# Low parts of 64 weight units: a subtraction on VectorE replaced by an adding transfer out of main memory

## The chip, the cores and the metric

One Trainium2 chip, one core. Its engines run side by side: TensorE (matmuls, PE in the profile), VectorE (DVE), ScalarE (ACT), GpSimd (POOL) and SyncE (SP), the last three also issuing transfers that 16 DMA engines carry out. The metric is the time of one execution in device microseconds; the kernel before takes 1455.31 us (median of three runs).

## The reference

One layer of an encoder for 256 tokens of width 2048, in float32: a normalisation, one wide input projection, two kinds of attention, two gates, two branch projections, an output projection, a gated MLP with a width-3 convolution, a gated extra embedding, and a last normalisation. Cut to its products:

```python
h = rms_norm(x, attn_norm)
qa, ka, va, qb, kb, vb, ga, gb = split(h @ w_in)
ya, yb = windowed_gqa(qa, ka, va), dilated_attention(qb, kb, vb)
x = x + (sigmoid(ga) * (ya @ w_branch_a) + sigmoid(gb) * (yb @ w_branch_b)) @ w_out
hf = rms_norm(x, ffn_norm)
x = x + (gelu(dwconv(hf @ w_ffn_gate)) * (hf @ w_ffn_up)) @ w_ffn_down
x = x + sigmoid(rms_norm(x, ple_norm) @ w_ple_gate) * (p @ w_ple_proj)
return rms_norm(x, final_norm)
```

## The kernel before

**Weights as pieces and units.** All weights lie in main memory as `wts`: 258 pieces of 128 x 2048 float32 (1 MB each), in the order of their use. SyncE loads a piece into one of three `raw` buffers (`load`, L257; L254 and L255 for pieces of which one quarter was prepared earlier). A piece is cut into units, most of them of 1024 columns. `produce` turns a unit into two float32r tiles: a high part `hi`, which is the weights rounded by ScalarE (L305), and a low part `lo`, the weights minus `hi`, by VectorE (L306). Products are then made in three matmuls (`thirds`, L408 to L410): activations high by weights high, high by low, low by high. So a low part is first needed by the L409 matmul of its unit.

**Kinds of pieces.** `_PIECES` gives each a letter. `f`: 16 blocks of 128 x 128, used in the input projection (stage A) and in the MLP's two up-projections (E0, E1). `s`: two chunks by two column ranges, used in eight products, two units. `w`: the same with four chunks of one column range, also two units. `S` and `Z`: the same data used in seven products (a Strassen-like scheme), four units, two of them (ring `v`) being differences that VectorE makes in place in `raw` (L282, L283, L295 to L297).

**Stages behind attention.** In order: B0 to B3 (gates), each followed by ba (w_branch_a, two `w` pieces) and bb (w_branch_b, one `w` piece); D0, D1 (w_out); E0, F00, F01 (the MLP's first half: up-projections, then w_ffn_down for two column halves); E1, F10, F11 (its second half); pp0, pp1 (w_ple_proj); G0, G2, G3 (w_ple_gate). Pieces: B0 is `ssssSsSs`; B1 to B3, D0 and D1 are `SsSsSsSs`; F00 and F01 `ZZsZsZsZsZs`; F10 and F11 `ZsZsZsZsZss`; G0 `ZsZsZsZs`; G2 and G3 are `w` pieces; pp0 and pp1 one `s` piece each.

**Order.** Units go through two rings, six of kind `u` and two of kind `v`. When TensorE has used a unit for the last time, `drop` gives its place free and `pump` produces the next units in order. A planner at build time then fixes each engine's instruction order by the expected readiness of instructions; `keep` pins an instruction behind what its engine was given before. At the start of a stage VectorE and ScalarE also finish the stage before (L890 to L894, L1005, L1007, L1009; turning back of rows, L512 and L513).

**GpSimd's queue** holds little: in E0 and E1, transfers that prepare quarters of `Z` pieces (`ahead`: 52 loads of 384 KB, L268, and 52 stores of 128 KB, L275), and three square roots (L528) for the normalisations.

Of the kernel before, what the change touches and what calls it, by code (L numbers as in the profile page):

```python
# [10 lines left out]
F32 = mybir.dt.float32  # L11
FR = mybir.dt.float32r
AF = mybir.ActivationFunctionType
ALU = mybir.AluOpType
# [149 lines left out]
_PIECES, _STAGES = _pieces()  # L164
# [3 lines left out]
def _unit_list():  # L168

    units, of = [], []  # L170
    for p, (kind, _) in enumerate(_PIECES):
        if p == 0:
            cuts = [("n", a * P, b * P) for a, b in ((0, 1), (1, 4), (4, 7), (7, 11), (11, PIECE))]
        elif kind == "Z":
            cuts = [("n", WIDE, 2 * WIDE), ("n", 2 * WIDE, 4 * WIDE), ("T21", 0, 2 * WIDE), ("T03", 2 * WIDE, 4 * WIDE)]
        elif kind == "S":
            cuts = [("n", 0, WIDE), ("n", 2 * WIDE, 4 * WIDE), ("T13", 0, 2 * WIDE), ("T24", 2 * WIDE, 4 * WIDE)]
        else:
            cuts = [("n", 0, 2 * WIDE), ("n", 2 * WIDE, 4 * WIDE)]
        of.append(list(range(len(units), len(units) + len(cuts))))  # L180
        units += [(p, *cut) for cut in cuts]
    return units, of


_UNITS, _UNITS_OF = _unit_list()
_FBLOCKS = [(u, o) for p, (kind, _) in enumerate(_PIECES) if kind == "f" for u in _UNITS_OF[p]
            for o in range((_UNITS[u][3] - _UNITS[u][2]) // P)]
_LAST_OF = {u: o for u, o in _FBLOCKS}
# [5 lines left out]
def _encoder(ctx: ExitStack, tc, xt, pt, xrow, cols, gainrow, table, onehot, mask, ident_in, wts, out):  # L194
    nc = tc.nc
# [12 lines left out]
    def bank(which, *shape):  # L208

        if which in RING:  # L210
            n = turns.get(which, 0)
            turns[which] = n + 1
            which = RING[which][n % len(RING[which])]
        else:
            which = BANK[which]
        return ps.tile(list(shape) or [P, 2 * T], F32, name="bank", tag="b%d" % which, bufs=1)
# [33 lines left out]
    def load(r, a=0, b=PIECE):  # L250
        if a == 0:
            raws[r] = wpool.tile([P, PIECE * P], F32, name="raw", bufs=3)
        if _PIECES[r][0] == "Z":
            nc.sync.dma_start(raws[r][:, WIDE:], wts[r][:, WIDE:])  # L254
            nc.sync.dma_start(raws[r][:, :WIDE], ahead.pop(r))  # L255
        else:
            nc.sync.dma_start(raws[r][:, a * P:b * P], wts[r][:, a * P:b * P])  # L257
        state["raw"] = r + 1
# [20 lines left out]
    def sums_of_weights(raw):  # L279

        q = [raw[:, i * WIDE:(i + 1) * WIDE] for i in range(4)]
        nc.vector.tensor_tensor(q[1], q[0], q[1], op=ALU.subtract)  # L282
        nc.vector.tensor_tensor(raw[:, 2 * WIDE:], raw[:, 2 * WIDE:], view(q[0], 0, (0, 2), (1, WIDE)), op=ALU.subtract)  # L283

    def produce():

        u = state["unit"]
        p, kind, a, b = _UNITS[u]
        while state["raw"] < min(p + 3, _NPIECES):
            load(state["raw"])  # L290
        raw = raws[p]
        ring = "u" if kind == "n" else "v"
        if kind == "T13":
            q = [raw[:, i * WIDE:(i + 1) * WIDE] for i in range(4)]
            nc.vector.tensor_tensor(raw[:, :2 * WIDE], raw[:, WIDE:3 * WIDE], raw[:, :2 * WIDE], op=ALU.subtract)  # L295
            nc.vector.tensor_tensor(q[2], q[2], q[0], op=ALU.subtract)
            nc.vector.tensor_tensor(q[3], q[3], q[2], op=ALU.subtract)  # L297
        behind = _PIECES[p][0] == "Z" == _PIECES[p - 1][0]
        if kind == "T21" and not behind:
            sums_of_weights(raw)  # L300
        src = raw[:, a:b]
        pool = wpool if ring == "u" else held["tok"]
        hi = pool.tile([P, b - a], FR, name=ring + "h", bufs=RINGS[ring])
        lo = pool.tile([P, b - a], FR, name=ring + "l", bufs=RINGS[ring])
        nc.scalar.activation(hi, src, AF.Copy)  # L305
        nc.vector.tensor_tensor(lo, src, hi.bitcast(F32), op=ALU.subtract)  # L306
        if behind and u == _UNITS_OF[p][1]:
            sums_of_weights(raw)
        made[u] = (hi, lo)
        state["unit"] = u + 1  # L310
        state[ring] -= 1

    def pump():
        while not state["early"] and state["unit"] < len(_UNITS):
            p, kind = _UNITS[state["unit"]][:2]
            if state["u" if kind == "n" else "v"] <= 0 or kind != "n" and "tok" not in held:
                break
            produce()

    def weights(u):  # L320
        while state["unit"] <= u:
            produce()
        return made[u]
# [167 lines left out]
    keep = tc.keep_in_program_order  # L491
# [148 lines left out]
    for step in order:  # L640
        if len(step) == 3:
            produce()
        else:
            for k in range(*step):
                gained(hs[:, k, :], x[:, k, :], gain(0, k))
            ready = step[1]
        while state["at"] < min(FIRST * ready, _EARLY[state["unit"]]):
            k, e = divmod(state["at"], FIRST)
            block(firsts[e], hs[:, k, :], k == 0, k == KC - 1)
        while 4 * done + 9 < state["at"] // FIRST:  # L650
            square(done)
            done += 1
# [16 lines left out]
    b = bank("misc", NH, 2 * T)  # L669
# [470 lines left out]
    for half in range(2):  # L1140
# [3 lines left out]
        stage = "E%d" % half  # L1144
# [87 lines left out]
    for t in range(2):  # L1232
        for h in range(2):
            cols = slice(3 * WIDE + h * T, 3 * WIDE + (h + 1) * T)
            u, r = c[t][:, WIDE + h * T:WIDE + (h + 1) * T], xr[:, t, cols]
# [72 lines left out]
```

## Time and profile before

| | |
|---|---|
| runs | 1454.77, 1455.31, 1455.72 us |
| span of the profiled execution, first to last instruction | 1453.7 us |
| TensorE busy, matmuls | 1442.7 us (99%) |
| VectorE busy | 1220.8 us (84%) |
| ScalarE busy | 829.6 us (57%) |
| GpSimd busy | 73.8 us (5%) |
| granted TensorE clock, mean | 0.997 |
| mean transfer rate | 213 GB/s |
| read from main memory | 299.94 MB |

The profile is one execution on the chip; for it only the span is recorded, and the runs' times hold 1.6 us more than that span at their median, which lies around the instructions. "Busy" is the time in which at least one instruction of an engine runs. Lines such as L306 are lines of the kernel. In rows of a timeline stand the start in us, the duration in us, the engine, the line, the operation, output and inputs, and in brackets the idle time before it with what ended it. In the list of waits stand the total, the count and the longest. In the windows stand the stretch, its length and each engine's busy time with its count, then the granted clock, the share of the DMA engines and GB/s.

### The profile page before, as it was taken

What the parts mean: (1) busy time and instruction counts of PE and PEld (TensorE: products, weight loads), DVE (VectorE), ACT (ScalarE), POOL (GpSimd) and SP (SyncE); (2) the same over time, 40 slices, a digit from 0 to 9 for tenths busy, and PEclk for the clock granted to TensorE, in tenths of its full rate; (3) what the DMA queues carried; (4) which work ended last, traced back from release to release, by engine and by line L of the source; (5) the groups of instructions that cost most, each with busy time, mean ns of one, the idle gap of its engine ahead of it and who ended that gap; (6) DMA issues with size and microseconds to landing.
All of it is one profiled execution on the core that took longest, in us unless ns stands there. A gap on an engine that the chain in (4) does not pass through costs nothing.

```text
span 1453.7 us, 19747 instructions
## 1 busy us (share of the span) xinstructions
PE 1442.7 (99%) x7470; PEld 1234.0 (85%) x7470; DVE 1220.8 (84%) x1730; ACT 829.6 (57%) x1148; POOL 73.8 (5%) x113
## 2 busy tenths in 40 slices
PE   9999999999999999999999999999999999999997
PEld 8888888888888888888888888888888888888885
DVE  7677665679998989989877999997878799998994
ACT  7455544546555656566545566465545466555753
POOL 0000000000000000000221100000121200000000
PEclk9999999999999999999999999999999999999998
DMA  9753445435456456465767655566776765556462
GB/s 330 252 209 146 155 167 175 172 143 203 189 190 231 180 210 239 178 253 203 277 238 267 241 208 198 189 248 227 263 275 243 271 236 213 197 194 233 173 236 82
DMA packets 58522, 310.17 MB, mean 213 GB/s; under 512 B 7028, under 2 KB 12020, under 8 KB 29500
## 3 DMA queue, kind: packets, MB, share of 16 engines
q1 hardware_dynamic: 49388, 280.46, 53.1%
q0 software_dynamic: 8320, 27.27, 5.2%
q8 instruction: 58, 0.95, 0.3%
q10 hardware_dynamic: 720, 1.19, 0.2%
q14 instruction: 36, 0.29, 0.1%
HBM read 299.94 MB, written 8.95 MB: 212 GB/s over the span
## 4 chain that ended last, share of the span: by engine, by line
PE 98%; DMA 0%; issue 0%; DVE 0%; ACT 0%; SPq 0%; POOLq 0%; POOL 0%; DVEq 0%
PE bank L351 29%; PE bank L358 15%; PE bank L408 15%; PE bank L409 14%; PE bank L410 14%; PE bank L397 2%; PE bank L399 2%; PE bank L398 2%; PE bank L335 2%; PE bank L336 1%; PE bank L939 1%; PE bank L755 0%; PE bank L703 0%; PE bank L702 0%; PE bank L701 0%; DMA raw<-in_wts 0%
## 5 line engine op out<-in xcount | busy, mean ns | idle before, releaser
L305 ACT ACTIVATE uh<-raw 128x1024 fp32r<-128x1024 f32 (+2 forms) x519 | 518.1, 1010 | 297.0 <-PE bank L410 106.5
L306 DVE TENSOR_TENSOR ul<-raw,uh 128x1024 fp32r<-128x1024 f32 (+2 forms) x519 | 594.4, 1164 | 96.5 <-ACT uh L305 65.9
L351 PE MATMUL bank<-hf,uh 128*128 128x512 f32 x1408 | 336.3, 391 | 0.0
L351 PEld LDWEIGHTS bank<-hf,uh 128*128 128x128 f32 x1408 | 258.9, 188 | 50.1
L358 PEld LDWEIGHTS bank<-hf,ul 128*128 128x128 f32 x1408 | 180.4, 191 | 6.7
L358 PE MATMUL bank<-hf,ul 128*128 128x256 f32 x1408 | 182.8, 283 | 0.0
L305 ACT ACTIVATE vh<-raw 128x1024 fp32r<-128x1024 f32 x96 | 101.1, 1058 | 59.8 <-DVE raw L282 27.0
L306 DVE TENSOR_TENSOR vl<-raw,vh 128x1024 fp32r<-128x1024 f32 x96 | 116.3, 1220 | 1.1
L351 PE MATMUL bank<-hs,uh 128*128 128x512 f32 x432 | 103.6, 392 | 0.0
L351 PEld LDWEIGHTS bank<-hs,uh 128*128 128x128 f32 x432 | 79.5, 188 | 15.6
L410 PE MATMUL bank<-uh,act 128*128 128x512 f32 x218 | 84.9, 390 | 0.0
L409 PE MATMUL bank<-ul,act 128*128 128x512 f32 x218 | 84.8, 389 | 0.0
L408 PE MATMUL bank<-uh,act 128*128 128x512 f32 x218 | 84.6, 390 | 0.0
L496 ACT ACTIVATE t<-bank 128x256 f32<-128x256 f32 x122 | 45.3, 374 | 59.8 <-PE bank L358 48.7
L408 PE MATMUL bank<-uh,hs 128*128 128x512 f32 x172 | 67.4, 392 | 0.0
L410 PE MATMUL bank<-uh,hs 128*128 128x512 f32 x172 | 67.2, 391 | 0.0
L409 PE MATMUL bank<-ul,hs 128*128 128x512 f32 x172 | 67.0, 389 | 0.0
L1084 ACT ACTIVATE gw<-gw,cl 128x256 f32<-128x256 f32 x44 | 24.0, 594 | 72.2 <-DVE gw L1081 71.9
L271 DVE TENSOR_TENSOR ahead<-ahead 128x256 f32<-128x256 f32 x52 | 21.9, 422 | 46.8 <-DMA ahead<-in_wts 46.8
L268 POOL DMA_DIRECT2D ahead<-in_wts x52 | 39.0, 750 | 375.7 <-DMA ahead<-ahead 207.0
L358 PE MATMUL bank<-hs,ul 128*128 128x256 f32 x432 | 56.6, 284 | 0.0
L358 PEld LDWEIGHTS bank<-hs,ul 128*128 128x128 f32 x432 | 54.5, 191 | 1.0
(266 smaller groups left out, 2423.8 us busy)
## 6 DMA issues: line engine op xcount, KB each, us to landing
raw<-in_wts SPq DMA_DIRECT2D x225, 1024.0 KB, 4.9
ahead<-in_wts POOLq DMA_DIRECT2D x52, 384.0 KB, 5.2
raw<-in_wts SPq DMA_DIRECT2D x26, 768.0 KB, 5.1
ahead<-ahead POOLq DMA_DIRECT2D x52, 128.0 KB, 4.4
raw<-ahead SPq DMA_DIRECT2D x26, 256.0 KB, 4.9
raw<-in_wts SPq DMA_DIRECT2D x12, 512.0 KB, 7.0
xr<-in_xrow SPq DMA_DIRECT2D x4, 512.0 KB, 8.4
x<-in_xt SPq DMA_DIRECT2D x13, 128.0 KB, 6.0
```

The lines of the kernel that those rows point to most:

```text
L268: keep(nc.gpsimd.dma_start(q, wts[p][:, :3 * WIDE].rearrange("p (q c) -> p q c", c=WIDE)[:, :, cols]))
L305: nc.scalar.activation(hi, src, AF.Copy)
L306: nc.vector.tensor_tensor(lo, src, hi.bitcast(F32), op=ALU.subtract)
L335: nc.tensor.matmul(acc, hi[:, w], m, start=first, stop=False, skip_group_check=True)
L351: nc.tensor.matmul(acc, weights(u)[0][:, o * P:(o + 1) * P], m, start=first, stop=False, skip_group_check=True)
L358: nc.tensor.matmul(acc[:, T:], weights(u)[1][:, o * P:(o + 1) * P], m[:, :T], start=False, stop=last, skip_group_check=True)
L397: nc.tensor.matmul(acc[:, :n * P], xh, hi, start=(k == 0), stop=False)
L398: nc.tensor.matmul(acc[:, :n * P], xh, lo, start=False, stop=False)
L408: nc.tensor.matmul(acc, sh, wh, start=first, stop=False)
L409: nc.tensor.matmul(acc, sh, wl, start=False, stop=False)
L410: nc.tensor.matmul(acc, sl, wh, start=False, stop=last)
L496: keep(nc.scalar.activation(t, acc[:, T:], AF.Copy, scale=scale))
```

## The change

The second unit (columns 1024 to 2047) of every `s` and `w` piece in the stages B, ba, bb, D, F and G0 is treated in another way, 64 units in all. ScalarE writes the negated rounding of the weights into the low part's tile, and then the rounding into the high part's tile. A transfer issued by GpSimd then reads the same 1024 columns (512 KB) once more out of main memory and adds them to what is in the low part's tile. VectorE's subtraction falls away for them. All other units stay as they were, and so do all matmuls.

```diff
+_MOVED = {_UNITS_OF[p][1] for stage in _STAGES if stage[0] in "BbDFG" and stage not in ("G2", "G3")
+          for p in _STAGES[stage] if _PIECES[p][0] in 'sw'}
...
         hi = pool.tile([P, b - a], FR, name=ring + "h", bufs=RINGS[ring])
         lo = pool.tile([P, b - a], FR, name=ring + "l", bufs=RINGS[ring])
-        nc.scalar.activation(hi, src, AF.Copy)
-        nc.vector.tensor_tensor(lo, src, hi.bitcast(F32), op=ALU.subtract)
+        if u in _MOVED:
+            nc.scalar.activation(lo, src, AF.Copy, scale=-1.0)
+            nc.scalar.activation(hi, src, AF.Copy)
+            keep(nc.gpsimd.dma_start(lo, wts[p][:, a:b], accum_op=ALU.add))
+        else:
+            nc.scalar.activation(hi, src, AF.Copy)
+            nc.vector.tensor_tensor(lo, src, hi.bitcast(F32), op=ALU.subtract)
```

## The prediction, made before the changed kernel ran

> **What bounds the kernel now.** I read the page first, then TensorE's list of waits, then the windows of the stages that the change touches, then the times of single units. The page:
>
> ```profile
> span 1453.7 us, 19747 instructions
> PE 1442.7 (99%) x7470; PEld 1234.0 (85%) x7470; DVE 1220.8 (84%) x1730; ACT 829.6 (57%) x1148; POOL 73.8 (5%) x113
> PEclk9999999999999999999999999999999999999998
> PE 98%; DMA 0%; issue 0%; DVE 0%; ACT 0%; SPq 0%; POOLq 0%; POOL 0%; DVEq 0%
> ```
>
> The chain that ended last is TensorE for 98% of the span. A busy TensorE may hide short waits, since ends of matmuls are modelled, so the list of waits and the starts count:
>
> ```profile
> PE bank L234 <- DVE mhalf L229: 1.1, 1, 1.1
> PE bank L336 <- DVE ul L306: 0.2, 1, 0.2
> ...
> 402.15 0.39 PE L409 MATMUL bank<-ul,hs 128*128 128x512 f32 x1
> 402.38 0.39 PE L410 MATMUL bank<-uh,hs 128*128 128x512 f32 x1
> 402.60 0.39 PE L408 MATMUL bank<-uh,S 128*128 128x512 f32 x1
> ```
>
> Two waits in the whole execution, 1.3 us together, both before the touched stages; and in them one 512-column matmul starts 0.23 us after the last. Nothing that makes VectorE lighter can bring much: there is hardly a wait to take away. What can change the time is a new wait. The touched stages are gates and branch projections (B, ba, bb), w_out (D), the two w_ffn_down stages (F) and the first w_ple_gate stage (G0):
>
> ```profile
> 350.00:620.00 270.00, 270.00 (x1208) 221.13 (x1207) 254.28 (x304) 163.19 (x187) 0.00 (x0) 1.00 0.54 199
> 850.00:985.00 135.00, 135.00 (x632) 112.63 (x631) 126.00 (x143) 78.61 (x93) 0.00 (x0) 1.00 0.56 207
> 1225.00:1400.00 175.00, 175.00 (x800) 145.06 (x799) 162.86 (x202) 107.77 (x138) 1.08 (x1) 1.00 0.57 206
> ...
> 620.00:850.00 230.00, 230.00 (x1314) 202.49 (x1313) 194.28 (x320) 130.82 (x196) 32.63 (x49) 1.00 0.69 249
> ```
>
> Columns: PE, PEld, DVE, ACT, POOL busy, clock, DMA share, GB/s. VectorE is busy 543 of 580 us there, ScalarE 350, GpSimd 1.1. The fourth row is the first MLP stage, untouched, where GpSimd's own transfers run today.
>
> **The change part by part.** By the piece patterns, 64 units move: 18 in B, 8 in ba, 4 in bb, 8 in D, 22 in F, 4 in G0.
>
> *Removed:* 64 subtractions on VectorE of 1.22 us (next start 1.14 us later). 64 x 1.14 = 73 us off its 543. On TensorE's path that is worth 0 by the waits above. I do not count the few short delays among them.
>
> *Added on ScalarE:* 64 rounded negations of 1.05 us, 67 us on 350, so it is busy 72%. The negation comes first, where the rounding stood, so the low part's first half is ready when the high part was; the high part comes 1.05 us later. The piece's buffer is free after two ScalarE passes instead of one pass and a lagging subtraction, so SyncE's next load does not start later.
>
> *Added to the DMA engines:* 64 x 512 KB = 33.6 MB in 580 us, 58 GB/s on about 203. In proportion to the share that is 0.55 to 0.71 as plain transfers; the first MLP stage ran at 0.69 and 249 GB/s with no wait of TensorE. So bandwidth is no bound; latency may be.
>
> *Added wait:* TensorE's first low-part matmul of such a unit waits for a transfer instead of VectorE, and all later matmuls stand behind it. The path is: negation ends, GpSimd's queue issues, the data comes and is added, TensorE may read. Before has no adding transfer. The nearest rows are GpSimd's transfers in the MLP stages:
>
> ```profile
> L268 POOL DMA_DIRECT2D ahead<-in_wts x52: 741/743/929, 638.8 to 1168.4; - x52
> DMA to landing us min/median/max: 3.3/4.8/6.5
> ...
> ahead<-in_wts POOLq DMA_DIRECT2D x52, 384.0 KB, 5.2
> ahead<-ahead POOLq DMA_DIRECT2D x52, 128.0 KB, 4.4
> ```
>
> From 128 to 384 KB costs 0.8 us, so 0.4 us per 128 KB over a fixed 4.0 (one of the two is a store, so this is rough). A plain 512 KB would take 4.0 + 1.6 = 5.6 us. Adding must also read what lies in the destination: if that doubles the moving part, 7.2; if it triples it, 8.8. Below, 4.8, the median over both kinds. I take 6.0, nearest to the plain row, because the DMA share is 0.55 in these stages and 0.69 where the row was taken. Ends kept: 4.8 and 8.8.
>
> The Trainium skill, page "DMA: Bandwidth & Descriptors", section "Anatomy of one DMA — SWDGE (gpsimd) path", fits a transfer from GpSimd as 2.0 us plus its bytes at 436 GB/s, which is 3.2 us for 512 KB (an estimate by that page); by it no unit below would be late and the sum is 0. The trace disagrees on its own case: the fit gives 2.9 us for the 384 KB that took 5.2.
>
> *Cover:* how long after the end of the rounding (in the changed kernel, of the negation) TensorE first needs the low part. I matched ScalarE's L305 roundings in order to units, and units to TensorE's matmuls. The tightest and the widest of the 64, one in the steady run of stage B, and those that decide:
>
> ```profile
> 947.07 1.04 ACT L305 ACTIVATE uh<-raw 128x1024 fp32r<-128x1024 f32 x1
> 951.63 0.39 PE L409 MATMUL bank<-ul,act 128*128 128x512 f32 x1
> ...
> 302.52 1.06 ACT L305 ACTIVATE uh<-raw 128x1024 fp32r<-128x1024 f32 x1 [0.75 <-PE bank L351]
> 318.60 0.39 PE L409 MATMUL bank<-ul,hs 128*128 128x512 f32 x1
> ...
> 441.42 1.06 ACT L305 ACTIVATE uh<-raw 128x1024 fp32r<-128x1024 f32 x1 [0.45 <-PE bank L410]
> 452.33 0.39 PE L409 MATMUL bank<-ul,hs 128*128 128x512 f32 x1
> ...
> 605.72 0.46 ACT L512 ACTIVATE hf<-bank,cl 128x256 fp32r<-128x256 f32 x1
> 606.07 1.05 ACT L305 ACTIVATE uh<-raw 128x1024 fp32r<-128x1024 f32 x1
> 612.37 0.39 PE L409 MATMUL bank<-ul,merged 128*128 128x512 f32 x1
> ...
> 889.57 1.04 ACT L305 ACTIVATE uh<-raw 128x1024 fp32r<-128x1024 f32 x1
> 895.54 0.39 PE L409 MATMUL bank<-ul,act 128*128 128x512 f32 x1
> ...
> 1310.16 1.04 ACT L305 ACTIVATE uh<-raw 128x1024 fp32r<-128x1024 f32 x1
> 1315.70 0.39 PE L409 MATMUL bank<-ul,act 128*128 128x512 f32 x1
> ...
> 1357.47 1.08 ACT L305 ACTIVATE uh<-raw 128x1024 fp32r<-128x1024 f32 x1
> 1365.16 0.39 PE L409 MATMUL bank<-ul,pl 128*128 128x512 f32 x1
> ```
>
> Covers: 3.5 us (second F stage), 15.0, 9.9, 5.3 (D1), 4.9 (first F stage), 4.5 (fourth F stage), 6.6 (G0). Stage B and D0 in the steady run lie near 10: the ring of six units sets that, and 6.0 fits in. The short ones lie behind the start of a stage, where VectorE is late with sums:
>
> ```profile
> 920.66 0.69 DVE L306 TENSOR_TENSOR ul<-raw,uh 128x512 fp32r<-128x512 f32 x1 [1.79 <-ACT uh L305]
> ...
> 939.34 4.09 DVE L306 TENSOR_TENSOR ul<-raw,uh 128x1024 fp32r<-128x1024 f32 x4
> 943.35 0.69 DVE L282 TENSOR_TENSOR raw<-raw 128x512 f32<-128x512 f32 x1
> ```
>
> VectorE has no pause from 920.66 on, and the second of the four subtractions at 939.34 is of a moved unit. Without it the sums at 943.35, on which ScalarE's next units wait, come 1.14 us sooner. So the 3.5 becomes 4.66; in the first F stage one moved unit stands ahead likewise, 4.93 + 1.14 = 6.07; in the fourth F stage two, 4.5 + 2.28 = 6.8. The D1 unit sits behind ScalarE's L512 and gets nothing, 5.25; nor does the one in G0.
>
> *Sum at 6.0 us:* short by 1.34 in the second F stage and 0.75 in D1, other units not at all: +2.1 us. The profiled span becomes 1455.8. The median of the runs, 1455.31, lies 1.6 us above the span of 1453.7 (the start and end outside it), so the forecast is 1457.4. The limit of what can be told from no change is 0.2%, 2.9 us: I forecast no change that can be told, on its slow side.
>
> *Queues:* GpSimd has 1.1 us of work in these stages. The one other instruction that could meet a transfer there is the root before G0, quoted in the rivals. SyncE's loads are not moved past anything.
>
> **The rivals.**
>
> *Slower, the transfers land late.* The same units, a larger price. At 7.2 us: 2.54 + 1.95 + 1.13 + 0.42 + 0.6 (G0) = 6.6 us, 1462. At 8.8 the same five are short by 4.1, 3.6, 2.7, 2.0 and 2.2, and some units with covers of 7.4 to 8.6 by another 4: 18.6, 1474. It decides from 6.3 us on (1.64 + 1.05 + 0.23 = 2.9). For it: an addition needs the destination read too, on DMA engines that are busy more than half of the time. Against: one late unit gives the next one its delay as cover, and the order on TensorE is made by a planner that pulls high-part products ahead of a late low part. Above 10 us the steady covers break too, 64 us for each further us: 1540 at 11, with little chance.
>
> *Slower, GpSimd's queue is blocked.*
>
> ```profile
> 1361.30 1.08 POOL L528 TENSOR_TENSOR rr<-rv,mhalf 128x2 f32<-128x2 f32 x1 [183.86 <-DVE rv L526]
> ```
>
> GpSimd stands on this root's wait for 184 us. If the planner leaves it ahead of G0's first transfer, that can be issued at 1362.4 instead of 1358.6 and lands 6.0 later, 3.2 us after the use at 1365.16: 1460.6 with the sum. Against: in program order that unit is produced first. A rule of the Trainium skill points the same way for all 64: "SBUF — State Buffer", section "Who interferes with whom", says VectorE in its 2-port modes locks GpSimd out while descriptors are written. The issue times above (741 to 929 ns over 52, beside a VectorE busy 84%) show no such lock; at most one 1.2 us VectorE instruction per transfer, which is the 7.2 us case.
>
> *Hidden anyway.* At 4.8 only the unit in the second F stage is short, by 0.1: 1455.4. The fastest transfer, 3.3, speaks for it; against it, half of the transfers take longer than 4.8, and they are smaller and add nothing. (By the skill's fit above it would be this case, too.)
>
> *Faster.* VectorE's 73 us end waits that the modelled ends hide. It would take 2.9 us of them; the regular starts and the 0.2 us in the list speak against. 1452.
>
> **How the numbers follow.** Forecast (landing between 4.9 and 6.3) 0.40, hidden 0.10, late transfers 0.38, blocked queue or above 10 us 0.07, faster 0.05. Same 0.50, slower 0.45, faster 0.05. The likeliest is 1457.4. The range goes from 1454.0 (hidden, with 1.3 us gained) to 1470.0 (a landing of 8.3 us), leaving out about 1 in 10 above and less below. The forecast alone reaches from 1455 to 1458.2.
>
> **What would show it.** L306's subtractions fall from 519 to 455, L305's line splits, GpSimd gets 64 issues with a time to landing near 6 us, VectorE's busy time falls by about 73 us, ScalarE's rises by about 67. TensorE's waits name transfers into ul, a few times, about 1 us each, at 606 to 620 and 945 to 955, and none in stage B. It is wrong if stage B shows waits (landing above 10), if many of the F units do (above 8), if the clock falls from 1.00 in the touched windows, or if waits appear on high parts, which would be ScalarE's added 67 us.

## The result, and the profile after

The changed kernel takes 1556.96 us (median of 1555.10, 1556.96 and 1562.67) against 1455.31: ratio 1.0705, 95% interval 1.0676 to 1.0734. That is 101.6 us slower, far above the range of 1454.0 to 1470.0. Lines stand lower in it: L305 is now L312 (the two ScalarE passes of a moved unit are L308 and L309), L306 is L313, L408 to L410 are L415 to L417, and the new transfer is L310. The page of the changed kernel:

```profile
span 1553.3 us, 19981 instructions
PE 1472.7 (95%) x7470; PEld 1245.6 (80%) x7470; DVE 1155.1 (74%) x1666; ACT 886.1 (57%) x1212; POOL 129.4 (8%) x177
PEclk9999999999999999899999999989999999999999
...
raw<-in_wts SPq DMA_DIRECT2D x225, 1024.0 KB, 5.5
ul<-in_wts POOLq DMA_DIRECT2D x64, 512.0 KB, 9.3
...
raw<-in_wts SPq DMA_DIRECT2D x26, 768.0 KB, 8.3
```

The span grew by 99.6 us. TensorE, with the same 7470 matmuls, is busy 30.0 us longer (1472.7 against 1442.7) and pauses 69.6 us more (1553.3 - 1472.7 = 80.6 against 11.0). VectorE lost 65.7 us of work and ScalarE gained 56.5: neither total matters. The three last rows tell where to look: the new transfers take 9.3 us from issue to landing, and SyncE's loads also land later than before. Their rows on the page of the kernel before:

```profile
raw<-in_wts SPq DMA_DIRECT2D x225, 1024.0 KB, 4.9
...
raw<-in_wts SPq DMA_DIRECT2D x26, 768.0 KB, 5.1
```

What TensorE waited for in the changed kernel:

```profile
PE bank L416 <- DMA ul<-in_wts: 57.0, 26, 6.7
PE bank L415 <- DVE c L899: 5.4, 2, 2.8
PE bank L946 <- DVE merged L950: 4.5, 4, 1.9
```

Before, that list had 1.3 us in two waits. Now the landing alone ends 57.0 us in 26. Most of the rest ends with sums on VectorE, at the starts of stages above all.

The other 30 us are TensorE working more slowly. Windows over the gate and branch stages, over two of the worst places and over one untouched stage, columns as before (clock, DMA share and GB/s last):

```profile
350.00:620.00 270.00, 252.09 (x1094) 201.65 (x1093) 202.49 (x249) 167.77 (x190) 24.40 (x28) 0.99 0.81 242
...
630.00:680.00 50.00, 37.42 (x161) 29.88 (x160) 29.82 (x35) 22.99 (x29) 1.75 (x2) 0.86 0.62 196
980.00:1030.00 50.00, 41.25 (x169) 33.09 (x168) 36.62 (x39) 26.93 (x29) 3.45 (x4) 0.93 0.60 183
1060.00:1290.00 230.00, 230.00 (x1322) 203.18 (x1322) 190.09 (x315) 126.78 (x188) 35.48 (x54) 1.00 0.71 253
```

The granted clock falls to 0.86 and 0.93 where the longest pauses are and is 1.00 where there are none. In the clock records of the whole run the rate is 0.5 in 12 stretches ahead of the last one at the end, each of 3.41 or 6.83 us, 51.2 us together; work at half rate for that long costs 25.6 us. The Trainium skill's page "TensorE: Matmul & The Clock Gate", section "Part 1: The HAM clock gate (the "warmup" mystery)", says that TensorE drops to half rate after an idle window of about 3.4 us; the trace agrees in the length of the stretches, but no whole idle window is needed: every stretch begins within 5.2 us of the start of a wait, and six of the twelve waits are of only 1.9 to 2.8 us.

By stage (the shift of the same matmul between the two traces), the loss is 25.2 us in B0 to D0, 21.0 in D1, 21.8 in F00 and F01, 21.1 in F10 and F11, 10.4 in G0, and 0 in E0, E1, G2 and G3.

One late unit, the second of D1, in the timeline of the changed kernel:

```profile
618.40 1.07 ACT L309 ACTIVATE uh<-raw 128x1024 fp32r<-128x1024 f32 x1
...
623.55 1.22 DVE L313 TENSOR_TENSOR ul<-raw,uh 128x1024 fp32r<-128x1024 f32 x1
...
625.56 1.05 ACT L308 ACTIVATE ul<-raw 128x1024 fp32r<-128x1024 f32 x1
626.63 0.92 SPq L259 DMA_DIRECT2D raw<-in_wts  x2
627.01 0.86 POOL L310 DMA_DIRECT2D ul<-in_wts  x1 [18.56 <-DVE vl L313]
...
637.05 0.79 PE L416 MATMUL bank<-ul,merged 128*128 128x512 f32 x1 [6.74 <-DMA ul<-in_wts]
```

The negation runs 7.2 us after the rounding, not before it: it comes behind VectorE's subtraction for the first half (623.55). The transfer is issued 0.4 us after the negation, but 0.4 us behind the issue of a 1 MB load. Its first packet moves at 631.24, 4.2 us after the issue, the last ends at 636.69, and the landing is told at 637.00. TensorE stands for 6.74 us, and its next matmul takes 0.79 instead of 0.39 us: half rate.

### The profile page after: what moved, and what is told of

Same layout as the page of the kernel before. It is cut to its first block, busy times and chain, and to the rows that moved or that the text cites. A ratio compares the mean times of both kernels' runs of the same rounds, so it can differ in the third digit from the quotient of the medians.

```text
span 1553.3 us, 19981 instructions
## 1 busy us (share of the span) xinstructions
PE 1472.7 (95%) x7470; PEld 1245.6 (80%) x7470; DVE 1155.1 (74%) x1666; ACT 886.1 (57%) x1212; POOL 129.4 (8%) x177
## 5 line engine op out<-in xcount | busy, mean ns | idle before, releaser
L313 DVE TENSOR_TENSOR ul<-raw,uh 128x1024 fp32r<-128x1024 f32 (+2 forms) x455 | 520.5, 1157 | 229.1 <-ACT uh L312 196.4
L312 ACT ACTIVATE uh<-raw 128x1024 fp32r<-128x1024 f32 (+2 forms) x455 | 453.0, 1005 | 367.1 <-PE bank L417 126.5
L310 POOL DMA_DIRECT2D ul<-in_wts x64 | 55.9, 874 | 955.5 <-ACT ul L308 488.8
L313 DVE TENSOR_TENSOR vl<-raw,vh 128x1024 fp32r<-128x1024 f32 x96 | 116.9, 1221 | 23.8 <-ACT vh L312 23.1
L312 ACT ACTIVATE vh<-raw 128x1024 fp32r<-128x1024 f32 x96 | 100.4, 1052 | 33.3 <-DVE raw L284 12.7
L416 PE MATMUL bank<-ul,act 128*128 128x512 f32 x218 | 90.4, 415 | 24.6 <-DMA ul<-in_wts 24.6
L417 PE MATMUL bank<-uh,act 128*128 128x512 f32 x218 | 88.4, 407 | 0.0
L415 PE MATMUL bank<-uh,act 128*128 128x512 f32 x218 | 87.5, 405 | 0.0
L416 PEld LDWEIGHTS bank<-ul,act 128*128 128x128 f32 x218 | 42.9, 197 | 38.9 <-DMA ul<-in_wts 30.0
L308 ACT ACTIVATE ul<-raw 128x1024 fp32r<-128x1024 f32 x64 | 67.2, 1049 | 7.1 <-PE bank L416 4.5
L415 PE MATMUL bank<-uh,hs 128*128 128x512 f32 x172 | 68.8, 400 | 0.0
L309 ACT ACTIVATE uh<-raw 128x1024 fp32r<-128x1024 f32 x64 | 66.9, 1045 | 2.8 <-PE bank L358 2.5
L417 PE MATMUL bank<-uh,hs 128*128 128x512 f32 x172 | 68.1, 397 | 0.0
```

The source lines that it names most:

```text
L308: nc.scalar.activation(lo, src, AF.Copy, scale=-1.0)
L310: keep(nc.gpsimd.dma_start(lo, wts[p][:, a:b], accum_op=ALU.add))
L415: nc.tensor.matmul(acc, sh, wh, start=first, stop=False)
L416: nc.tensor.matmul(acc, sh, wl, start=False, stop=False)
L417: nc.tensor.matmul(acc, sl, wh, start=False, stop=last)
```

## The experiments

Times are compared with runs of the kernel before on the same chip (medians of 1455.1 to 1455.4). Diffs are against the changed kernel. Theory 1 in the expectations is that the landing of an adding transfer is longer than I took it; the others are told where they stand.

**Leaving out one part at a time.** ScalarE's two passes with VectorE's subtraction kept and no transfer:

```diff
-            keep(nc.gpsimd.dma_start(lo, wts[p][:, a:b], accum_op=ALU.add))
+            nc.vector.tensor_tensor(lo, src, hi.bitcast(F32), op=ALU.subtract)
```

> The negation and both ScalarE passes stay, but the low part is then subtracted by VectorE as before, and there is no transfer. Theory 1: no loss, 1455 to 1457 us. Theory 3 (ScalarE's added 67 us delay high parts and the buffers' release, and so the loads): a good part of the 100 us stays, over 1480 us.

Measured 1456.71 us, ratio 1.0010 (1.0000 to 1.0019). So the added ScalarE work is hidden, as predicted, and the loss lies with the transfers.

The same transfers, overwriting instead of adding (the low part then is the weights themselves, the difference is left out):

```diff
-            keep(nc.gpsimd.dma_start(lo, wts[p][:, a:b], accum_op=ALU.add))
+            keep(nc.gpsimd.dma_start(lo, wts[p][:, a:b]))
```

> The 64 transfers overwrite the low part's tile with the weights instead of adding to it; all else as in the changed kernel (the output is then not the reference's: the low parts of these units hold whole weights). Theory 1 (the addition is what is slow: 0.63 us per round of 4 KB packets, where plain ones take 0.16): landing falls from 9.3 to about 5 to 5.6 us, TensorE's waits on these transfers from 57 us to under 5, the time to 1455 to 1459 us. Theory 2 (the conversion to float32r or GpSimd's path itself is slow at 512 KB): landing stays at 8 to 10 us and the time above 1530 us.

Measured 1509.78, ratio 1.0371 (1.0338 to 1.0404). Its list of waits, and its row of the transfers:

```profile
PE bank L416 <- DMA ul<-in_wts: 23.8, 11, 5.3
```

```profile
ul<-in_wts POOLq DMA_DIRECT2D x64, 512.0 KB, 6.8
```

The adding is worth 47 us of the 101.6. A plain transfer lands 2.5 us sooner and still costs 54, so the addition is not the only term that was missed.

**Is main memory the slow part of an adding transfer?** The same addition with the weights taken from the `raw` buffer:

```diff
-            keep(nc.gpsimd.dma_start(lo, wts[p][:, a:b], accum_op=ALU.add))
+            keep(nc.gpsimd.dma_start(lo, src, accum_op=ALU.add))
```

> The adding transfer reads the weights from the raw buffer in SBUF instead of main memory. If the round of 0.63 us is the addition's own (theory 1), the transfer takes as long, 8 to 10 us to land, and the time is no better than 1555 us, worse if the buffer, held until the transfer has read it, delays the next load. If main memory's latency in the second read is what is slow, the landing falls to 5 to 6 us.

A single run took 1565.09 us. The landing is 8.2 us at the median, and a packet of 4 KB takes 327 ns with either source, where a plain one takes 159 (GpSimd's loads in the kernel before) to 174. So the source isn't what makes a packet slow. That the whole became no faster has a reason of its own: each `raw` buffer is now held until the landing. SyncE stands on these transfers 64 times there, 452.9 us in all, before it can issue a load.

**Less to move, or a later use.** Half of the columns by the transfer, the other half by VectorE:

```diff
-            nc.scalar.activation(lo, src, AF.Copy, scale=-1.0)
+            nc.scalar.activation(lo[:, WIDE:], src[:, WIDE:], AF.Copy, scale=-1.0)
...
-            keep(nc.gpsimd.dma_start(lo, wts[p][:, a:b], accum_op=ALU.add))
+            keep(nc.gpsimd.dma_start(lo[:, WIDE:], wts[p][:, a + WIDE:b], accum_op=ALU.add))
+            nc.vector.tensor_tensor(lo[:, :WIDE], src[:, :WIDE], hi[:, :WIDE].bitcast(F32), op=ALU.subtract)
```

> Only columns 512 to 1023 of each moved unit go by negation and adding transfer (256 KB), VectorE subtracts the other 512; rings as in the changed kernel. Theory 1: eight rounds of 2 KB packets, half the moving time, landing 6 to 7 us, as the plain transfers of 512 KB, so a time near theirs, 1500 to 1520 us. If packets cost the same whatever their size, landing stays near 9 us and the time near 1555 us.

Measured 1515.82, ratio 1.0417 (1.0376 to 1.0458), landing 7.3 us. Half of the bytes take away 2.0 us of the landing and 41 us of the loss. And the moved unit used in the last four of its piece's eight products, but for a stage's last piece:

```diff
                     t, n, c = g // 4, g // 2 % 2, g % 2
+                    if us[1] in _MOVED and i < len(pieces) - 1:
+                        c, t, n = g // 4, g // 2 % 2, g % 2
```

> In the eight-product pieces, but for the last of a stage, the moved unit is used in the last four products instead of every second one, so its low part is needed about 3 x 0.68 = 2.0 us later. Theory 1 with its corollary (a fixed landing against a fixed cover): the stalls in B and D0 of 0.5 to 1 us per unit vanish and those behind stage starts shrink by 2 us each: 1500 to 1520 us. Theory 4 (the DMA engines cannot supply the weights fast enough): TensorE waits in sum as long as now, 1545 to 1560 us.

Measured 1540.53, ratio 1.0580 (1.0562 to 1.0597), 44.1 us of waits on the landing in 25. That is 16 us less, and above what theory 1 gave. Not every unit got the 2 us: in three units the negation now comes 10.0 to 12.4 us after the rounding (at most 8.8 in the changed kernel). So the run agrees with landing against cover as the sum, but it is no clean step of the cover.

**Does the negation hang on VectorE through the ring?** The moved low parts get a ring of two of their own, the others keep four:

```diff
-        lo = pool.tile([P, b - a], FR, name=ring + "l", bufs=RINGS[ring])
+        if ring == "u" and u in _MOVED:
+            lo = pool.tile([P, b - a], FR, name="ml", bufs=2)
+        else:
+            lo = pool.tile([P, b - a], FR, name=ring + "l", bufs=4 if ring == "u" else RINGS[ring])
```

> The moved units' low parts get a ring of their own (two places, the other low parts four; six in all as before). Theory 5 (the low parts' places are given out in order of the units, so a negation stands behind VectorE's late subtraction of the first half and loses the cover that the rounding had): negations start where their roundings do, the waits behind stage starts (D1 +21 us, F01 +16, F11 +13) shrink by more than half, and the time falls to 1490 to 1515 us; what is left is landing of 9.3 us against covers of 5 to 10. Theory 1 alone (only the landing is too long): no change, 1550 to 1560 us.

> As the last, and the transfer overwrites instead of adding (the output is then not the reference's: these low parts hold whole weights). Theories 1 and 5 together: landing near 6.8 us against the covers that I had read from the roundings, 1458 to 1466 us. If neither holds (loads late, ScalarE, clock), the 1510 us of the plain transfers stay.

> The kernel before with its low parts' ring split four and two, no transfer and no negation. It prices the split itself: 1455 to 1460 us by both theories.

Measured 1589.24 (ratio 1.0927, 1.0907 to 1.0946) adding, 1531.85 (1.0526, 1.0504 to 1.0548) overwriting, and 1477.00 (1.0152, 1.0136 to 1.0168) for the split ring with VectorE's subtraction and no transfer. Of the adding one:

```profile
PE bank L419 <- DMA ml<-in_wts: 67.5, 22, 6.9
PE bank L368 <- DVE ul L316: 11.9, 12, 2.1
```

My gain did not come. In three units the negation had been 4.8 to 8.8 us behind the rounding, and two of them had stalled, the D1 unit above for 6.7 us. Now their negation comes first and none of the three stalls (issue to landing 5.5 us each); in all, 11 negations come behind their rounding where 29 did. So the ring has a part in their order. But two places are too few: a branch piece's unit now has its negation 6.2 to 6.4 us behind the rounding and stalls 5.1 to 6.8 us, four times, and the split alone costs 22 us. Less the control, adding still loses 112 us and overwriting 55. The run frees one wait and makes another, so it doesn't price this step.

**Do the stages add up, and what do transfers cost that nobody waits for?** First, only B, ba, bb and D0 are moved, 34 units:

```diff
-_MOVED = {_UNITS_OF[p][1] for stage in _STAGES if stage[0] in "BbDFG" and stage not in ("G2", "G3")
+_MOVED = {_UNITS_OF[p][1] for stage in _STAGES if stage[0] in "Bb" or stage == "D0"
```

> Only the second halves of the gate and branch stages and of the first w_out stage are moved; the second w_out stage, the four w_ffn_down stages and G0 are as before. Theory A (each late unit costs its own stall, stage by stage): the changed kernel lost 4.7 + 6.1 + 4.9 + 6.1 + 3.4 = 25.2 us in these stages and the other 74 elsewhere, so 1480, 1475 to 1485. Theory B (the transfers load the chip as a whole, through the clock or later loads, and the short covers only show it): the loss goes with the number of transfers, 34 of 64, about half of 101 us, 1505 or more.

Measured 1484.59, ratio 1.0205 (1.0190 to 1.0220): 29.4 us, of which 25.2 by the matmuls' shift in the moved stages, the sum that the changed kernel loses there, and 4.8 in D1, the stage behind. Theory A. Then the idle transfers; VectorE subtracts as before:

```diff
-            nc.scalar.activation(lo, src, AF.Copy, scale=-1.0)
             nc.scalar.activation(hi, src, AF.Copy)
-            keep(nc.gpsimd.dma_start(lo, wts[p][:, a:b], accum_op=ALU.add))
+            nc.vector.tensor_tensor(lo, src, hi.bitcast(F32), op=ALU.subtract)
+            if "sink" not in state:
+                state["sink"] = dram.tile([P, 2 * WIDE], FR, name="sink")
+                keep(nc.gpsimd.dma_start(state["sink"], hi))
+            else:
+                keep(nc.gpsimd.dma_start(state["sink"], hi, accum_op=ALU.add))
```

> VectorE subtracts as before. Beside it, 64 transfers of 512 KB by GpSimd add each moved unit's finished high part onto a buffer in main memory that nobody reads; they start when the high part is rounded. ScalarE has no negation. So the DMA work is there, and nobody waits for its landing. Theory A (the loss is TensorE waiting for the landing): 1455 to 1459. Theory B (the transfers delay SyncE's loads, seen as raw loads at 8.3 instead of 5.1 us in the changed kernel, and ScalarE and TensorE wait for those): 20 us or more are lost, 1475 to 1510, with waits of ScalarE on raw loads.

> As the run before, but the transfers overwrite the idle buffer instead of adding. Theory A: 1455 to 1457. Theory B: about half of what the adding ones lose, 1465 to 1485.

Measured 1476.61 (ratio 1.0147, 1.0130 to 1.0164) adding, and 1462.80 (1.0052, 1.0037 to 1.0067) overwriting. Of the adding one, the page's transfers and ScalarE's wait for loads (the profiled execution was 10 us above the median):

```profile
raw<-in_wts SPq DMA_DIRECT2D x225, 1024.0 KB, 5.6
sink<-uh POOLq DMA_DIRECT2D x64, 512.0 KB, 8.0
...
raw<-in_wts SPq DMA_DIRECT2D x26, 768.0 KB, 6.8
```

```profile
ACT uh L316 <- DMA raw<-in_wts: 117.4, 67, 5.5
```

In the kernel before, ScalarE's wait for loads was:

```profile
ACT uh L305 <- DMA raw<-in_wts: 41.5, 35, 3.0
```

Theory B has a share: no wait of TensorE ends with these transfers, yet 21.4 us go (7.6 without the addition), through loads that land later and a ScalarE that waits for them. Ten times, 15.1 us together, ScalarE waits for an idle transfer itself, which holds the high part's place until it has read it; the changed kernel has no such wait. Also, these transfers read on the chip and write to main memory, the other way round. So 21 is a rough size for this share in the changed kernel and not its exact part.

**The negation and the transfer first.** Before the first half of a touched piece is rounded, the second half's place is taken, its negation done and its transfer issued; two places must be free for that:

```diff
+        if u + 1 in _MOVED:
+            a2, b2 = _UNITS[u + 1][2:]
+            lows[u + 1] = pool.tile([P, b2 - a2], FR, name=ring + "l", bufs=RINGS[ring])
+            nc.scalar.activation(lows[u + 1], raw[:, a2:b2], AF.Copy, scale=-1.0)
+            keep(nc.gpsimd.dma_start(lows[u + 1], wts[p][:, a2:b2], accum_op=ALU.add))
...
-            if state["u" if kind == "n" else "v"] <= 0 or kind != "n" and "tok" not in held:
+            if state["u" if kind == "n" else "v"] <= (state["unit"] + 1 in _MOVED) or kind != "n" and "tok" not in held:
```

> The negation and the adding transfer of a moved second half are issued ahead of its first half's rounding and subtraction; to that end both units of the piece need a free place in the ring of six at once. Theory A1 (the covers fell because the negation came behind VectorE's subtraction of the first half): the negation comes some 2 to 5 us earlier against the use, the landing of 9.3 us is covered in most units, 1475 to 1520. Theory A2 (waiting for two places makes the units start a place later, as the split ring did): the pieces start later and TensorE waits on first halves too, 1560 or more.

Measured 1494.76, ratio 1.0273 (1.0246 to 1.0300): 62 of the 101.6 us are back. Its row of the page, its summary of the tile, and its waits on the landing:

```profile
ul<-in_wts POOLq DMA_DIRECT2D x64, 512.0 KB, 5.6
```

```profile
DMA to landing us min/median/max: 5.3/5.6/11.0
```

```profile
PE bank L424 <- DMA ul<-in_wts: 9.3, 4, 3.8
```

Two things happened, and I had expected only the first. The negation stands ahead of its own unit's rounding in 60 of 64 units (in the changed kernel it comes after it in 29). And the landing fell from 9.3 to 5.6 us though the bytes and the addition are the same: issued this early, most transfers go out well before SyncE issues the next load. Only 23 of the 64 have their first packet later than 1.8 us after the issue (37 in the changed kernel), and 37 land within 5.3 to 5.7 us, the next load being issued 1.5 us or more behind them. Now it is the load that comes second, and its landing stays above the 4.9 and 5.1 us of the kernel before:

```profile
raw<-in_wts SPq DMA_DIRECT2D x225, 1024.0 KB, 5.5
...
raw<-in_wts SPq DMA_DIRECT2D x26, 768.0 KB, 6.7
```

What are the 39.6 us that are left: the two places, or the transfers? The run just told (e16 in the expectations) was changed in two ways: without negation and transfer, VectorE subtracting, and with overwriting (difference left out again). The first, as a diff against the run just told:

```diff
-            nc.scalar.activation(lows[u + 1], raw[:, a2:b2], AF.Copy, scale=-1.0)
-            keep(nc.gpsimd.dma_start(lows[u + 1], wts[p][:, a2:b2], accum_op=ALU.add))
...
+            nc.vector.tensor_tensor(lo, src, hi.bitcast(F32), op=ALU.subtract)
```

> VectorE subtracts all low parts as before, with no negation and no transfer; only the order of e16 is kept, in which both units of a touched piece need a free place at once. Theory A3 (the 39.5 us that e16 still loses are the transfers: their contention with the loads, 21 us in the idle adding run, and the four stalls left): 1455 to 1462. Theory A2 (they are the price of waiting for two places): 1475 to 1495.

> The order of e16, with transfers that overwrite the low part instead of adding onto it. Theory A3: the idle overwriting run lost 7.6 us and a plain transfer lands sooner, so 1460 to 1470. Theory A2: as e16 less a little, 1480 to 1492.

Measured 1455.75 (ratio 1.0004, 0.9995 to 1.0014) and 1475.19 (1.0144, 1.0126 to 1.0161). Waiting for two places costs nothing, so the 39.6 us come with the transfers and their negations. The control has no negation ahead of the first half's rounding, where one pass of 1.05 us now stands; what that pass costs without a transfer was not run. The overwriting run is 5 us above what I gave it. In it only 1.4 us of TensorE's waits end with a landing. ScalarE waits 94.1 us for loads there, against 35.3 in the control, so most of its 20 us seem to come by the late loads; that is more than the 7.6 of the idle run.

All together, in us over the kernel before:

| | adding | overwriting |
|---|---|---|
| idle, nobody waits | 21.4 | 7.6 |
| issued first | 39.6 | 20.0 |
| as changed | 101.6 | 54.4 |
| no transfer: two ScalarE passes | 1.3 | |
| no transfer: order of "issued first" | 0.5 | |

No version was found that beats the kernel before, and none of the runs points to one: before, TensorE has 1.3 us of waits that a lighter VectorE could take away, and idle overwriting transfers alone cost 7.6.

## Why the prediction was wrong

**Landing: the term that was mis-sized.** I took 6.0 us, nearest to the plain row, with 8.8 as the upper end. Measured 9.3 at the median (5.4 to 11.6). My guess for a tripled moving part came near it in size, and its reason was wrong. By the packets' records the issue takes 0.87 us (plain 0.53) and the moving 5.2 us at the median (plain 3.4). In 37 of the 64 transfers the first packet comes 2.0 to 4.8 us after the issue; in 33 of these a weight load, issued before or at most 0.4 us behind, is still under way. In the other 27 the first packet comes after 1.6 to 1.7 us. But 21 of them then move for 6.0 to 7.5 us and land after 8.3 to 9.7; in 16 of these SyncE issues a load 0.6 us behind the transfer. Only six move undisturbed, in 3.5 to 3.9 us, and land after 5.4 to 5.8, less than I took. The overwriting transfers meet loads as often (34 late first packets) and land after 6.8. So neither the addition nor the meeting with a load makes 9.3 us alone; the two together do. A unit mostly becomes ready just when a load is issued, and my DMA share of 0.55, an average, could not show that they coincide. I had even set the lower share of these stages against the MLP stage as a reason for a small price. By the fit in the Trainium skill, page "DMA: Bandwidth & Descriptors", section "Anatomy of one DMA — SWDGE (gpsimd) path", it would be 3.2 us, an estimate; the fastest 512 KB transfer into the chip took 3.8 (overwriting, in the run with a ring of its own), and only idle ones out of the chip were faster, down to 2.9.

**"The negation comes first, where the rounding stood."** This failed in 29 of 64 units: the negation comes mostly 0.9 to 2.0 us after the rounding, and three times 4.8 to 8.8 us. And covers were shorter than those I read from the trace before. Measured from the end of the negation, the tight ones are 3.6 us in D1 (I had 5.25; there the negation did come first), 2.8 in the second F stage (4.66), 4.2 in the fourth (6.8) and 5.3 in G0 (6.6). Little of the relief of 1.14 us for each moved unit ahead is to be seen in the two F stages. Of the 57.0 us of waits, 37.8 fall on units whose negation is behind its rounding. If those had begun when their roundings did and had landed in the same time, at most some 25 us of waits would have gone (an estimate, the smaller of stall and lateness summed over these units). The run that issues the negation first, and its control, show this step and the meeting with loads to be worth 62 of the 101.6 us; they change both at once. Why the planner puts these negations behind is not shown; the run with a ring of its own shows only that the places of the ring have a part in it.

**"SyncE's next load does not start later", "bandwidth is no bound".** The mean share does not order the stalls: the worst windows have 0.60 and 0.62, below the 0.71 of an untouched stage without a wait. But my 0.71 for the touched stages held for plain transfers only: from 350 to 620 us the share is 0.68 in the overwriting run and 0.81 in the changed kernel, where a packet takes 327 instead of 174 ns. And the loads land later, 8.3 instead of 5.1 us for 768 KB, and later units hang on them. I had asked only whether the transfers wait for the loads, and not the reverse. Idle transfers lose 21 us (adding), a rough size for this.

**The clock.** I named a falling clock as a sign of error and gave it no price. Behind pauses of a few us it costs TensorE about 26 us by the clock records, of the 30 us that its busy time grew: waits of 70 became a loss of 100.

**"None in stage B."** I had read covers near 10 for the steady units. From the end of the negation the ten of them that stalled had 7.7 to 10.1, against 9.5 to 10.7 us from there to the landing; the waits come to 13.3 us in B to D0, and to 13.1 us in 9 in the run that moves only these. The prediction said that each us above 10 costs 64; the steady covers broke sooner, and by less.

**What held.** No run shows a gain from VectorE's relief (65.7 us of its busy time, where I had 73), though none has it without a transfer. ScalarE's added work, 56.5 us of busy time where I had 67, is hidden (1.3 us, at the edge of what can be told). The GpSimd queue is not blocked: the issue follows the negation by 0.3 to 0.4 us in all 64 and takes 0.85 to 1.05 us beside a VectorE that is busy 74%, so no lock by VectorE shows. The longest stalls fall in the stages that I named, 5.8 and 6.7 us in D1, 5.9 in the second F stage, 4.5 in the fourth, 3.9 in G0, so the tight covers were looked for in the right places. The rival "transfers land late" had the right mechanism; its 1474 at 8.8 left out the lost covers, the loads and the clock.

## What to carry to other kernels

Where a matmul's operand is to come by a transfer, its price is the time to landing at the moment of its issue: look at what the other queue moves just then, not at the mean share of the DMA engines. Read a cover from the order that the changed kernel will have: here 29 of 64 negations came out behind the rounding that they were written ahead of. And when TensorE has hardly a wait, every stall counts once as a wait and once more, here about 0.4 times, as halved clock behind it.

## What the runs showed of the hardware

- An adding transfer moves 4 KB packets in 327 ns, a plain one in 159 to 174; the adding ones take as long with the source in main memory as on the chip. Undisturbed, 512 KB from main memory land in 5.3 to 5.9 us adding and in 3.8 to 4.3 plain.
- In the changed kernel the first packet of a transfer from GpSimd's queue comes 2.0 to 4.8 us after the issue in 37 of 64 (2.0 to 4.2 in 34 of 64 plain ones), nearly always with a load of SyncE under way, and 1.6 to 1.7 us (1.2 to 1.3) after it in the others. The Trainium skill, page "DMA: Bandwidth & Descriptors", section "SWDGE vs HWDGE vs iDMA", says that a DMA engine takes turns between its queues; the late first packets here come as if they stood behind part of what the other queue had already been given. No run here tells whether the data or the descriptors are what waits.
- Issue of an adding transfer holds GpSimd for 0.87 us, of a plain one of the same size for 0.53.
